# Second runs of a head pair: waiting output products ahead of the scores, and the runs planned nearer to the first

## The chip, the core and the metric

The kernel runs on one core of one Trainium2 chip. The metric is the device time of one execution in microseconds (us). The core's engines work side by side, each through its own queue in program order: TensorE (PE, matrix products into PSUM), VectorE (DVE), ScalarE (ACT), GpSimd (POOL, here mostly an issuer of weight loads) and SyncE (SP, an issuer of the other DMAs). They wait for each other through semaphores.

## The reference

One layer of a decoder trunk over 512 tokens with 1024 channels. Cut to what matters:

```
xn   = rmsnorm(x)
proj = xn @ w_in            # aq ak av ag | bq bf bi bg | gate_a gate_b
# attention branch: 8 heads x 64, blocks of 256, causal, relative-position bias
ya = attention(rmsnorm(aq), rmsnorm(ak), av, rel_bias)
ya = (ya * silu(ag)) @ w_up_a
# recurrence branch: 4 heads, key size 128, value size 128
yb = hgrn2(silu(bq), (1 - lb) * sigmoid(-bf), bi, log_decay(bf))
yb = (rmsnorm(yb) * silu(bg)) @ w_up_b
h  = x + (sigmoid(gate_a) * ya + sigmoid(gate_b) * yb) @ w_out
h  = h + (p @ w_ple) * sigmoid(h @ w_ple_gate)
```

All of it is held to float32 accuracy. With 512 tokens there are two key blocks and up to three chosen ones, so that every earlier block is always chosen and the attention is plain causal attention.

## The kernel before, in words

The large products (`mm3` at line 293, `prod_tok` at line 423) are each made of three products of rounded halves: high by high, high by low, low by high. A projection to 128 channels over all tokens is 24 matmuls of 128x512 and fills one PSUM bank. PSUM has 8 banks in three pools: "mm" (3 banks: the projections, one tile of the scores of a first run, and the attention's output `o`), "a" (3 banks: the scores `s`, and the recurrence's output `hop`) and "g" (2 banks: `lpb`, `lpa`, `hds` of the recurrence). A projection that needs a bank of "mm" waits until the last reader of the bank's previous content is through.

The weights of each projection are loaded by POOL or SP, rounded by ACT (`wh`, line 276) and completed by DVE (`wl`, line 277), two projections ahead.

The list `ORDER` sets the order of the projections while attention and recurrence run between them: bg, ag (gates of the two branches, `silu_block`), bf and bq (the recurrence's decay and query, `head`), ga and gb (the merge gates). `bf2` is the projection `bf` of recurrence head 2, and so on.

The order of TensorE's work is written out by a planner in the kernel. It keeps a clock `now` that `tick` moves on by 0.227 us for each matmul of a projection, and lets side generators go on when their due time has come: `attention`, `recurrence`, `hgrn_out` and others. `cost` adds time to the clock without running anything that is due. TensorE executes in exactly this order; the order on DVE, ACT, POOL and SP is made by a scheduler from it.

The attention works on four pairs of heads (0 to 3). A pair has two runs: the first (`STEPS[0]`) has the scores of query blocks 0, 1 and 2, the second (`STEPS[1]`) those of query block 3, six matmuls of line 815. After a run's scores come the softmax (DVE line 832, ACT lines 834 and 836, the transposition at DVE line 839) and 16 stores and regroupings of the probabilities through SP (line 850). `PACE` is the planned distance from one run to the next. The bias tiles of the next pair are loaded by SP (line 880, `bias`). After the next pair's first scores come the output products `o` of the pair before (line 863).

The recurrence works head by head. `hgrn_gates` makes of `bf` and `bq` the decay sums, keys and queries; ACT line 508 and DVE lines 512, 515 and 517 read the bank of `bf`, line 517 (`hk`) last. `hgrn_intra` prepares the inputs `hx` on DVE and ACT, waits for a run of the attention (`beside_attention`) and then issues the block products `lpb` and `lpa` (lines 592, 597, 563) right behind that run's scores. `hgrn_out` puts the head's output products (`hop`, lines 678 and 680: seven matmuls over four chunks of 128 tokens, each of which the profile records twice, since they are not of the rounded type) into the list `hops` for heads 0 to 2. Before the change that list is emptied at one place, in `hgrn_intra` of the next head, directly ahead of its block products:

```
        yield from beside_attention()
        while hops:
            hops.pop()()
        lpb = bank("g", f"lpb{h}")...
```

Line 695 (DVE) and line 692 (ACT) then read `hop`.

Of the kernel before, what the change touches and what calls it, by code (L numbers as in the profile page):

```python
# [28 lines left out]
LEVELS = (16, 8, 4, 2, 1)  # L29

STEPS = ((0, 1, 2), (3,))
PACE = (19.5, 22.5)

HP = 2.5
H0 = 8.0
# [33 lines left out]
def hybrid_layer_kernel(  # L69
# [32 lines left out]
    def bank(tag, name):  # L102
        return psum.tile([128, 512], F32, tag=tag, bufs={"mm": 3, "g": 2, "a": 3}[tag], name=name)
# [34 lines left out]
    def cost(us):  # L138
        now[0] += us
# [18 lines left out]
    def held_from(us, insts, until=None):  # L158

        def later():  # L160
            for inst in insts if until not in done else []:
                held(inst)
            yield 0.0

        spawn(later(), us)
# [331 lines left out]
    hops = []  # L497
# [290 lines left out]
    def attention(qn, kn, va, sags, res):  # L788
        def place(qb, j):

            return {0: (j, 0), 1: (2, 256 * j), 2: (j, 128), 3: (j, 0)}[qb]

        def tiles(step):
            return 2 + (len(STEPS[step]) > 1)
# [3 lines left out]
        def scores(hp, step):  # L798
            (qh, ql), (kh, kl) = qn[hp], kn[hp]
            nt = tiles(step)  # L800

            sps = [bank("a", f"s{hp}{step}{i}") for i in range(nt)]
            extra = bank("mm", f"s{hp}{step}x") if nt > 2 else None

            def where(qb, j):
                b_, o = place(qb, j)
                return (extra, 0) if (qb, j) == (1, 1) else (sps[b_], o)

            for qb in STEPS[step]:
                nk = 128 * (qb + 1)  # L810
                for i in range(3):
                    for j in range(2):
                        js = slice(64 * j, 64 * j + 64)
                        b_, o = where(qb, j)
                        PE.matmul(b_[:, o:o + nk], (qh, ql, qh)[i][js, qb * 128:qb * 128 + 128], (kh, kh, kl)[i][js, :nk],
                                  start=(i == 0), stop=(i == 2))
            cost(sum(3 * max(0.107, (qb + 1) * 0.0538) for qb in STEPS[step]))
            return where

        def softmax(hp, step, T, where):  # L820

            nt = tiles(step)
            z = pb[:, Z0[step]:Z0[step] + nt].rearrange("p t f -> p (t f)").rearrange("p (b t f) -> p b t f", b=4, t=nt)
            with tc.high_priority(offset=AHEAD):
                left = [sum(place(qb, j)[0] == b for qb in STEPS[step] for j in range(2)) for b in range(nt)]
                for qb, j in [(qb, j) for qb in STEPS[step] for j in range(2)]:
                    b_, o = place(qb, j)
                    nk = 128 * (qb + 1)
                    p_ = pb[:, b_, o:o + nk]
                    st = unit("ps", f"ps{hp}{qb}{j}", shape=(128, 4))  # L830
                    s_, so = where(qb, j)
                    in_order(V.tensor_tensor_reduce(p_, s_[:, so:so + nk], T[j][:, nk - 1::-1], -1.0, 3e38,  # L832
                                                    OP.add, OP.min, st[:, 0:1]))
                    A.activation(p_, p_, AF.Exp, bias=st[:, 0:1], scale=-1.0, accum_out=st[:, 1:2])  # L834
                    V.reciprocal(st[:, 2:3], st[:, 1:2])
                    A.activation(p_, p_, AF.Copy, scale=st[:, 2:3])  # L836
                    left[b_] -= 1
                    if left[b_] == 0:
                        V.transpose(z[:, :, b_, :].rearrange("p b (n c) -> p b n c", c=32),  # L839
                                    pb[:, b_].rearrange("p (n b c) -> p b n c", b=4, c=32))  # L840
            return z

        def sorted_groups(step, z):

            nt = tiles(step)
            pt = pb[:, PT0[step]:PT0[step] + nt].rearrange("p t f -> p (t f)").rearrange("p (a t f) -> p a t f", a=4, t=nt)
            with tc.high_priority(offset=AHEAD):
                for a in range(4):
                    for b in range(4):
                        nc.sync.dma_start(pt[32 * b:32 * b + 32, a], z[32 * a:32 * a + 32, b])  # L850
            return pt.rearrange("p a t (n c) -> p a (t n) c", c=32)

        def out_values(hp, pts):

            o = bank("mm", f"o{hp}")
            for step, pt in enumerate(pts):
                for qb in STEPS[step]:
                    qs = slice(qb * 128, qb * 128 + 128)
                    for kb in range(qb + 1):
                        for j in range(2):  # L860
                            h0 = hp * 128 + 64 * j
                            b_, o0 = place(qb, j)
                            PE.matmul(o[64 * j:64 * j + 64, qs], va[kb][:, h0:h0 + 64], pt[:, :, 4 * b_ + o0 // 128 + kb, :],
                                      start=(kb == 0), stop=(kb == qb))
            cost(1.5)
            sag = sags[hp]
            V.tensor_tensor(sag, o, sag, op=OP.mult)
            h_ = unit("A", f"yah{hp}", R)
            l_ = unit("A", f"yal{hp}", R)
            split(h_, l_, sag)  # L870
            res.append((h_, l_))
            done.add(f"ya{hp}")
# [3 lines left out]
        def bias(hp):  # L876
            for j in range(2):
                t = unit("T", f"bias{hp}{j}")
                row = ed[2 * hp + j:2 * hp + j + 1, :]
                held(nc.sync.dma_start(t, bass.AP(tensor=row.tensor, offset=row.offset, ap=[[1, 128], [1, 512]])))  # L880
                T[hp, j] = t
# [10 lines left out]
        for n in range(len(steps) + 1):  # L892
            ahead = BIAS if 0 < n < len(steps) and steps[n][1] == 0 else 0.0
            if n >= 1:
                yield PACE[steps[n - 1][1]] - ahead
            if ahead:
                bias(steps[n][0])
                yield ahead
            if n < len(steps):
                hp, i = steps[n]  # L900
                where = scores(hp, i)
            if n >= 1 and steps[n - 1][1] == NS - 1:
                ho = steps[n - 1][0]
                while f"ag{ho}" not in done:
                    yield lambda: f"ag{ho}" in done
                out_values(ho, [pts.pop(n - NS + i_) for i_ in range(NS)])
            if n < len(steps):
                z = softmax(hp, i, [T[hp, 0], T[hp, 1]], where)
                if others:
                    parts.clear()  # L910
                    others.pop()()
                    for n_, p_ in enumerate(list(parts)):
                        held_from(16.0 + 2.0 * n_, [p_])
                pts[n] = sorted_groups(i, z)
            runs[0] += 1
# [84 lines left out]
    spawn(qk_norm("q", proj_tok(0, "aq", xh, xl), qgain[:, 0:1], qn))  # L1000
    spawn(qk_norm("k", proj_tok(1, "ak", xh, xl), kgain, kn))
    spawn(attention(qn, kn, va, sags, ya))
    def up(i, n, ys, name):
        ws = weight(w_up[n, i])
# [341 lines left out]
```

## Time and profile before

| | |
|---|---|
| median of 3 runs | 452.07 us (450.89 to 452.41) |
| the profiled execution: its own time | 452.42 us |
| its span, from the first to the last instruction | 450.6 us |
| TensorE busy | 445.8 us, 99% of the span |
| VectorE, ScalarE, GpSimd busy | 334.6, 289.7, 59.9 us |
| mean granted TensorE clock | 0.999 |
| HBM read and written | 48.74 and 4.98 MB |

In the profile's rows a start time counts from the first instruction; the number behind it is the duration. Durations on TensorE overlap: the 128x512 matmuls take 0.39 us each and start 0.227 us apart. What a matmul costs is thus the distance to the next one's start. On DVE and ACT too the next instruction starts up to 0.1 us before the end of the one before, so that sums are made from starts to starts.

### The profile page before, as it was taken

The page shows a single profiled execution, that of the slowest core. Times are in us where ns is not written, and L with a number is a line of the kernel's source. Part 1 is how long each engine was busy: PE and PEld are TensorE (multiplying, and loading weights), DVE is VectorE, ACT ScalarE, POOL GpSimd, SP SyncE. Part 2 cuts the span into 40 slices and gives each one's busy share as a digit, 9 for nine tenths or more (in the row PEclk, how much of TensorE's full clock was granted, in tenths as well). Part 3 has the DMA queues.
Part 4 walks back from the last instruction along what each step waited for, and adds up shares of the span by engine and source line. Part 5 has one row for each costly group of instructions (what it writes and reads, how often), then busy time and mean ns, then how long its engine had stood idle before and what let it go on. Part 6 is the DMA issues. An engine that isn't in the chain of part 4 may idle for free.

```text
span 450.6 us, 8536 instructions
## 1 busy us (share of the span) xinstructions
PE 445.8 (99%) x3192; PEld 376.2 (83%) x3192; DVE 334.6 (74%) x682; ACT 289.7 (64%) x561; POOL 59.9 (13%) x97
## 2 busy tenths in 40 slices
PE   9999999999999999999999999999999999999996
PEld 8888888888878888878887888878888888899996
DVE  5869494776899797949857775465479868999844
ACT  5958474746689988979857996784135434555421
POOL 1000100000000101010100000111210103325520
PEclk9999999999999999999999999999999999999999
DMA  8802424168594455171425444265551444312111
GB/s 265 317 1 94 141 93 129 48 219 197 167 215 127 159 134 178 46 203 49 142 93 155 140 135 148 70 197 149 184 173 47 168 145 143 129 47 95 49 47 48
DMA packets 32857, 59.53 MB, mean 132 GB/s; under 512 B 7088, under 2 KB 18736, under 8 KB 32816
## 3 DMA queue, kind: packets, MB, share of 16 engines
q0 software_dynamic: 9056, 32.51, 22.5%
q1 hardware_dynamic: 23616, 26.47, 20.4%
q8 instruction: 25, 0.41, 0.4%
q14 instruction: 16, 0.13, 0.1%
q10 hardware_dynamic: 144, 0.01, 0.0%
HBM read 48.74 MB, written 4.98 MB: 119 GB/s over the span
## 4 chain that ended last, share of the span: by engine, by line
PE 89%; DVE 5%; SPq 2%; DMA 1%; issue 1%; ACT 0%; DVEq 0%
PE h L293 10%; PE g L1210 9%; PE ga L293 9%; PE gb L293 7%; PE ub L293 5%; PE aq L423 5%; PE ak L423 5%; PE ua L293 5%; PE av L423 5%; PE bf L293 5%; PE bi L423 5%; PE bq L293 4%; PE bg L293 4%; PE ag L293 4%; PE pe L293 2%; SPq L850 2%
## 5 line engine op out<-in xcount | busy, mean ns | idle before, releaser
L276 ACT ACTIVATE wh<-wf 128x1024 fp32r<-128x1024 f32 (+1 forms) x70 | 67.0, 958 | 63.2 <-issue 9.8
L277 DVE TENSOR_TENSOR wl<-wf,wh 128x1024 fp32r<-128x1024 f32 (+1 forms) x70 | 76.8, 1097 | 38.0 <-ACT wh L276 35.7
L266 POOL DMA_DIRECT2D wf<-in_w_tr_dram x30 | 15.8, 528 | 170.5 <-DVE wl L277 115.4
L293 PE MATMUL ga<-xh,wh 128*128 128x512 f32 x64 | 25.3, 396 | 0.4 <-DVE bg3s L491 0.4
L293 PE MATMUL gb<-xh,wh 128*128 128x512 f32 x64 | 25.0, 391 | 0.0
L293 PE MATMUL ga<-xh,wl 128*128 128x512 f32 x64 | 24.9, 390 | 0.0
L293 PE MATMUL ga<-xl,wh 128*128 128x512 f32 x64 | 24.9, 389 | 0.0
L293 PE MATMUL gb<-xl,wh 128*128 128x512 f32 x64 | 24.9, 389 | 0.0
L293 PE MATMUL h<-mh,wh 128*128 128x512 f32 x64 | 24.9, 389 | 0.0
L293 PE MATMUL h<-ml,wh 128*128 128x512 f32 x64 | 24.9, 389 | 0.0
L293 PE MATMUL h<-mh,wl 128*128 128x512 f32 x64 | 24.9, 389 | 0.0
L293 PE MATMUL gb<-xh,wl 128*128 128x512 f32 x64 | 24.9, 389 | 0.0
L834 ACT ACTIVATE pb<-pb,ps 128x128 f32<-128x128 f32 (+3 forms) x32 | 17.6, 551 | 10.0 <-DVE ps L832 10.0
L832 DVE CUSTOM_DVE_ANT_0 pb<-s,bias 128x128 f32<-128x128 f32 (+3 forms) x28 | 12.8, 493 | 7.1 <-DMA bias<-in_ed_dram 4.8
L1187 ACT ACTIVATE sg<-sg 128x256 f32<-128x256 f32 x12 | 5.0, 414 | 20.2 <-DVE sg L1184 20.2
L836 ACT ACTIVATE pb<-pb,ps 128x128 f32<-128x128 f32 (+3 forms) x32 | 16.0, 550 | 0.0
L542 ACT ACTIVATE hx<-hx 128x512 f32<-128x512 f32 x24 | 14.9, 623 | 1.4 <-DVE hx L541 1.3
L266 POOL DMA_DIRECT2D wf<-in_w_up_dram x16 | 8.6, 538 | 52.2 <-DVE wl L277 32.2
L839 DVE STREAM_TRANSPOSE pb<-pb 128x512 f32<-128x512 f32 x20 | 13.8, 696 | 2.0 <-ACT pb L836 2.0
L266 POOL DMA_DIRECT2D wf<-in_w_tok_dram x8 | 4.4, 549 | 80.2 <-DVE wl L277 68.2
L293 PEld LDWEIGHTS ga<-xh,wh 128*128 128x128 f32 x64 | 12.0, 188 | 3.5 <-DVE bg3s L491 0.8
L293 PEld LDWEIGHTS ga<-xh,wl 128*128 128x128 f32 x64 | 12.0, 188 | 2.6
(958 smaller groups left out, 1434.9 us busy)
## 6 DMA issues: line engine op xcount, KB each, us to landing
wf<-in_w_tr_dram POOLq DMA_DIRECT2D x30, 512.0 KB, 4.2
wf<-in_w_tok_dram POOLq DMA_DIRECT2D x8, 512.0 KB, 3.6
wf<-in_w_up_dram POOLq DMA_DIRECT2D x16, 256.0 KB, 3.0
wf<-in_w_o_dram POOLq DMA_DIRECT2D x8, 512.0 KB, 3.8
wf<-in_w_g_dram POOLq DMA_DIRECT2D x8, 512.0 KB, 3.6
wf<-in_w_tok_dram SPq DMA_DIRECT2D x6, 512.0 KB, 7.6
pb<-pb SPq DMA_DIRECT2D x64, 48.0 KB, 2.9
bias<-in_ed_dram SPq DMA_DIRECT2D x8, 256.0 KB, 4.1
```

The source lines that it names most:

```text
L266: (G if len(wraw) >= FAR else nc.sync).dma_start(raw, ap)
L276: rounds[i] = A.activation(hi, wraw[i], AF.Copy)
L277: V.tensor_tensor(lo, wraw[i], hi.bitcast(F32), op=OP.subtract)
L293: dense.append(PE.matmul(ps, a[:, k, :], b[k], start=(n == 0), stop=(n == tot - 1)))
L423: dense.append(PE.matmul(banks[t], a[:, s_], b[:, kk, :], start=(k == 0 and i == 0), stop=(k == KD - 1 and i == 2)))
L542: A.activation(x, x, AF.Exp)
L832: in_order(V.tensor_tensor_reduce(p_, s_[:, so:so + nk], T[j][:, nk - 1::-1], -1.0, 3e38, OP.add, OP.min, st[:, 0:1]))
L834: A.activation(p_, p_, AF.Exp, bias=st[:, 0:1], scale=-1.0, accum_out=st[:, 1:2])
L836: A.activation(p_, p_, AF.Copy, scale=st[:, 2:3])
L839: V.transpose(z[:, :, b_, :].rearrange("p b (n c) -> p b n c", c=32), pb[:, b_].rearrange("p (n b c) -> p b n c", b=4, c=32))
L850: nc.sync.dma_start(pt[32 * b:32 * b + 32, a], z[32 * a:32 * a + 32, b])
L1210: dense.append(PE.matmul(dst[i], a[:, k], b, start=(m == 0 and i in (1, 6, 5)), stop=(m == 11), skip_group_check=i not in (1, 6, 5)))
```

## The change

Two edits. The planned distance from a pair's first run to its second goes from 19.5 to 18.0 us. And where a second run (`i` is 1) is about to issue its scores, the list `hops` is emptied first, so that waiting output products of the recurrence stand ahead of the scores instead of behind them.

```
-PACE = (19.5, 22.5)
+PACE = (18.0, 22.5)
...
             if n < len(steps):
                 hp, i = steps[n]
+                while i and hops:
+                    hops.pop()()
                 where = scores(hp, i)
```

What this does to the order, at the places of which the prediction speaks. TensorE, second run of pair 0, before: `bf2` is the projection, `s010` and `s011` the scores of the pair's two heads, `hop0` the output products of recurrence head 0, and behind the rows shown come the block products `lpb1`.

```order
L293 MATMUL bf2_1555<-xh7_485,wl25_1475 128x512
L815 MATMUL s010_1580<-kh0_1130,qh0_877 128x512
L815 MATMUL s011_1581<-kh0_1130,qh0_877 128x512
L815 MATMUL s010_1580<-kh0_1130,ql0_881 128x512
L815 MATMUL s011_1581<-kh0_1130,ql0_881 128x512
L815 MATMUL s010_1580<-kl0_1134,qh0_877 128x512
L815 MATMUL s011_1581<-kl0_1134,qh0_877 128x512
L678 MATMUL hop0_1616<-sc_93,biv0_393 128x128 x2
L680 MATMUL hop0_1616<-ha0_609,st0_1095 128x128
L678 MATMUL hop0_1616<-sc_93,biv2_396 128x128
L680 MATMUL hop0_1616<-ha0_609,st0_1095 128x128
```

The same place after, up to the scores:

```order
L293 MATMUL bf2_1555<-xh5_452,wl25_1475 128x512
L678 MATMUL hop0_1574<-sc_93,biv0_393 128x128 x2
L680 MATMUL hop0_1574<-ha0_609,st0_1095 128x128
L678 MATMUL hop0_1574<-sc_93,biv2_396 128x128
L680 MATMUL hop0_1574<-ha0_609,st0_1095 128x128
L678 MATMUL hop0_1574<-sc_93,biv2_396 128x128
L680 MATMUL hop0_1574<-ha0_609,st0_1095 128x128
L815 MATMUL s010_1582<-kh0_1130,qh0_877 128x512
L815 MATMUL s011_1583<-kh0_1130,qh0_877 128x512
```

And where the block of small products ends, after:

```order
L563 MATMUL lpa1_1619<-hx1_16_1491 32x16 x16
L293 MATMUL bf2_1555<-xh6_460,wh25_1474 128x512
L293 MATMUL bf2_1555<-xl6_461,wh25_1474 128x512
L293 MATMUL bf2_1555<-xh6_460,wl25_1475 128x512
L293 MATMUL bf2_1555<-xh7_485,wh25_1474 128x512
L293 MATMUL bf2_1555<-xl7_486,wh25_1474 128x512
L293 MATMUL bf2_1555<-xh7_485,wl25_1475 128x512
L293 MATMUL bq2_1737<-xh0_412,wh26_1516 128x512
```

The whole block (scores, `hop`, `lpb`, `lpa`) stands six matmuls earlier, `hop0` ahead of the scores, and the last six matmuls of `bf2` come behind the block. In pairs 1 and 2 it is the same: the block stands six matmuls earlier (in pair 1 the last three of `bf3` come behind it, in pair 2 it now falls between `ga1` and `gb6`). In pair 3 `hops` is empty, and only the scores move, by six matmuls. The next pair's first run stands where it stood, since the 1.5 us that the planner counts for `hop` now fall into the distance.

DVE, second run of pair 1, before. Line 832 is the softmax's first step, `hu3`, `ha3` and `hk3` are the gates of recurrence head 3, which read the bank of `bf3`:

```order
L832 ISA pb_70,ps131_2237<-s111_2224,bias11_1863 128x512
L832 ISA ps131_2237 128x1
L512 TENSOR_SCALAR hu3_2411<-bf3_2188 128x512
L515 SCALAR_TENSOR_TENSOR ha3_2407<-bf3_2188,ha3_2407 128x512
L835 RECIPROCAL ps130_2231<-ps130_2231 128x1
L540 TENSOR_TENSOR hx2_8_2438<-hu2_1784 128x32x8
L541 TENSOR_TENSOR hx2_8_2438<-hu2_1784 128x32x8
L540 TENSOR_TENSOR hx2_4_2456<-hu2_1784 128x64x4
L541 TENSOR_TENSOR hx2_4_2456<-hu2_1784 128x64x4
L835 RECIPROCAL ps131_2237<-ps131_2237 128x1
L517 TENSOR_TENSOR hk3_2416<-ha3_2407,bf3_2188 128x512
```

After, from the softmax's transpositions on; between line 832 and these rows there now stand 15 others, the reduction of head 1's output (line 315), `wl35` and line 512 among them, and lines 695 and 313 stand ahead of line 832:

```order
L839 STREAM_TRANSPOSE pb_70<-pb_70 128x4x128 x2
L571 COPY_PREDICATED s322_2097<-mkf_69,lpb2_2283 128x64
L543 TENSOR_TENSOR hx2_4_2450<-hk2_1789,hx2_4_2450 128x64x4
L548 TENSOR_TENSOR hx2_4_2450<-ha2_1780,hx2_4_2450 128x64x4
L543 TENSOR_TENSOR hx2_2_2468<-hk2_1789,hx2_2_2468 128x128x2
L548 TENSOR_TENSOR hx2_2_2468<-ha2_1780,hx2_2_2468 128x128x2
L643 TENSOR_TENSOR ha2_1780<-ha2_1780,hu2_1784 128x384
L515 SCALAR_TENSOR_TENSOR ha3_2413<-bf3_2188,ha3_2413 128x512
L517 TENSOR_TENSOR hk3_2422<-ha3_2413,bf3_2188 128x512
```

Line 517, the last reader of the bank of `bf3`, had 8 instructions between the softmax's first step and itself, and now has 24, both transpositions among them. In pair 0 `hk2` moved likewise.

SP, the bias loads for pair 1, before (the 32x384 stores are those of pair 0's first run, the 32x256 ones those of its second):

```order
L850 DMA pb_70<-pb_70 32x384 x16
L1172 DMA pb_70<-in_pT_dram 128x512
L880 DMA bias10_1861<-in_ed_dram 128x512
L880 DMA bias11_1863<-in_ed_dram 128x512
L850 DMA pb_70<-pb_70 32x256 x16
```

After:

```order
L850 DMA pb_70<-pb_70 32x384 x16
L1174 DMA pb_70<-in_pT_dram 128x512
L850 DMA pb_70<-pb_70 32x256 x16
L880 DMA bias10_1861<-in_ed_dram 128x512
L880 DMA bias11_1863<-in_ed_dram 128x512
```

The two bias loads of pair 1 went behind the 16 stores of pair 0's second run. Those of pairs 2 and 3 keep their places; POOL's order is unchanged.

## The prediction

> **What bounds the kernel now.** I read the page first, for the share of the engines, and then the table of who TensorE waited for.
>
> ```profile
> PE 445.8 (99%) x3192; PEld 376.2 (83%) x3192; DVE 334.6 (74%) x682; ACT 289.7 (64%) x561; POOL 59.9 (13%) x97
> ```
> ```profile
> PE warm L193 <- PEq L1334: 0.8, 1, 0.8
> PE ga L293 <- DVE bg3s L491: 0.4, 1, 0.4
> ```
>
> TensorE is busy for 445.8 of 450.6 us, and all its waits in the table are two: 0.8 us at the start and one in the middle. So nothing that makes the attention or the recurrence ready earlier can shorten the kernel: TensorE has the same products to do either way. The time can change in three ways only: by what the edges between products of different shape cost, by the one stall going, and by new stalls. The one stall, in TensorE's timeline:
>
> ```profile
> 242.57 0.39 PE L293 MATMUL ga<-xh,wl 128*128 128x512 f32 x1
> 243.36 0.50 PE L293 MATMUL ga<-xh,wh 128*128 128x512 f32 x1 [0.40 <-DVE bg3s L491]
> ```
>
> The next matmul was due at 242.57 + 0.227 = 242.80 and started at 243.36: 0.56 us lost.
>
> **Edges between shapes.** Second run of pair 0 on TensorE, and the output products of head 3, which already stand between two projections:
>
> ```profile
> 152.17 0.39 PE L293 MATMUL bf<-xh,wl 128*128 128x512 f32 x1
> 152.49 0.50 PE L815 MATMUL s<-kh,qh 64*128 64x512 f32 x2
> 152.82 0.40 PE L815 MATMUL s<-kh,ql 64*128 64x512 f32 x2
> 153.06 0.40 PE L815 MATMUL s<-kl,qh 64*128 64x512 f32 x2
> 153.39 0.71 PE L678 MATMUL hop<-sc,biv 128*128 128x128 f32 x4
> 153.94 0.39 PE L680 MATMUL hop<-ha,st 128*128 128x128 f32 x2
> 154.83 0.39 PE L680 MATMUL hop<-ha,st 128*128 128x128 f32 x2
> 155.15 0.43 PE L592 MATMUL lpb<-hx 128*32 128x64 f32 x16
> ```
> ```profile
> 290.48 0.39 PE L293 MATMUL ga<-xh,wl 128*128 128x512 f32 x1
> 290.71 0.60 PE L678 MATMUL hop<-sc,biv 128*128 128x128 f32 x4
> 291.15 0.39 PE L680 MATMUL hop<-ha,st 128*128 128x128 f32 x2
> 292.18 0.48 PE L293 MATMUL ga<-xh,wh 128*128 128x512 f32 x1
> ```
>
> Entering the scores costs 0.32 - 0.23 = 0.09 us at the last projection matmul and another 0.33 - 0.24 = 0.09 in the first pair of scores. From scores to `hop` it is 0.33 - 0.24 = 0.09 and, in the first four records, 0.55 against the 0.44 of head 3 (290.71 to 291.15): 0.11. From `hop` to `lpb` it is 0.32 against 0.22 for two records. From a projection to `hop`, at head 3, it is nothing: 0.23 is the regular step. So in the new order (projection, `hop`, scores, `lpb`) the edge from scores to `hop`, 0.20 us, falls away. The edge into the scores is bought by `hop` instead of the projection. The edge from scores to `lpb` has no row; I take the 0.10 of `hop` to `lpb`, with 0.0 and 0.2 as bounds from the other edges. That is -0.2 us in each of pairs 0, 1 and 2: **-0.6 us** (-0.3 to -0.9). Splitting `bf2` and `bf3` adds nothing: the block had one edge from and one to a projection already. In pair 3 only the scores move.
>
> **What moves in time.** In pair 1 the block starts 6 x 0.227 = 1.36 us earlier. `hop` takes 1.47 us (290.71 to 292.18), so the scores come 1.47 + 0.1 - 1.36 = 0.2 us later than before, `hop` and `lpb` earlier. But the end of `bf3` now lies behind the block. It moves by the block's length, about 4 us (`s`, `hop` and the edges make 2.66 us up to 155.15, and `lpb` with `lpa` follow), and in pair 0 that of `bf2` likewise. Their readers follow. Below are TensorE's turns for three projections that need a bank which those readers or the gate `bg2` give back, with the start of pair 1's second run, then DVE's rows, then SP's issues:
>
> ```profile
> 167.50 0.39 PE L293 MATMUL gb<-xh,wh 128*128 128x512 f32 x1
> 194.88 0.39 PE L293 MATMUL bf<-xh,wh 128*128 128x512 f32 x1
> 201.09 0.50 PE L815 MATMUL s<-kh,qh 64*128 64x512 f32 x2
> 215.42 0.39 PE L293 MATMUL gb<-xh,wh 128*128 128x512 f32 x1
> ```
> ```profile
> 154.60 0.68 DVE L832 CUSTOM_DVE_ANT_0 pb<-s,bias 128x512 f32<-128x512 f32 x1
> 160.61 0.67 DVE L517 TENSOR_TENSOR hk<-ha,bf 128x512 f32<-128x512 f32 x1
> 178.62 0.29 DVE L832 CUSTOM_DVE_ANT_0 pb<-s,bias 128x128 f32<-128x128 f32 x1 [2.21 <-PE s L815]
> 191.42 0.68 DVE L491 TENSOR_TENSOR bg2s<-bg2s,bg 128x512 f32<-128x512 f32 x1
> 202.53 0.68 DVE L832 CUSTOM_DVE_ANT_0 pb<-s,bias 128x512 f32<-128x512 f32 x1
> 206.42 0.67 DVE L517 TENSOR_TENSOR hk<-ha,bf 128x512 f32<-128x512 f32 x1
> 207.01 0.74 DVE L695 SCALAR_TENSOR_TENSOR bg1s<-hop,sm,bg1s 128x512 f32<-128x512 f32 x1
> 208.29 0.25 DVE L602 TENSOR_TENSOR s<-lpb,mkf 128x128 f32<-128x128 f32 x1
> 210.39 0.68 DVE L519 TENSOR_TENSOR ha<-ha,hu 128x512 f32<-128x512 f32 x1
> 212.26 0.70 DVE L839 STREAM_TRANSPOSE pb<-pb 128x512 f32<-128x512 f32 x1
> 213.65 1.36 DVE L523 TENSOR_TENSOR_SCAN hu<-onec,ha 128x128 f32<-128x128 f32 x4
> 214.93 1.20 DVE L277 TENSOR_TENSOR wl<-wf,wh 128x1024 fp32r<-128x1024 f32 x1
> 216.18 0.54 DVE L643 TENSOR_TENSOR ha<-ha,hu 128x384 f32<-128x384 f32 x1
> 228.31 0.29 DVE L832 CUSTOM_DVE_ANT_0 pb<-s,bias 128x128 f32<-128x128 f32 x1 [3.24 <-DMA bias<-in_ed_dram]
> 230.21 0.29 DVE L832 CUSTOM_DVE_ANT_0 pb<-s,bias 128x128 f32<-128x128 f32 x1 [1.60 <-DMA bias<-in_ed_dram]
> ```
> ```profile
> 159.93 2.56 SPq L850 DMA_DIRECT2D pb<-pb  x4
> 163.16 0.90 SPq L880 DMA_DIRECT2D bias<-in_ed_dram  x2
> 165.87 10.75 SPq L850 DMA_DIRECT2D pb<-pb  x16
> 224.01 1.06 SPq L880 DMA_DIRECT2D bias<-in_ed_dram  x2
> ```
>
> **`gb5` behind `hk3`.** Three projections later `gb5` takes the bank of `bf3`. Before, line 517 ended at 206.42 + 0.67 = 207.09 for a turn at 215.42: 8.3 us to spare. Now its place on DVE is behind nearly everything that filled the idle-free stretch from 202.53 to 214.93. Of these 12.4 us, lines 695 and 313 (207.01 to 208.29, 1.3) now lie ahead of line 832, and line 519 (0.6) and the four scans (1.3) stay behind line 517. New ahead of it are a `wl` (1.15) and line 643 (0.5) with a small reduction (0.1). Line 517 therefore ends about 12.4 - 1.3 - 1.9 + 1.8 = 11.0 us after line 832 starts. Lines 695 and 313 now follow `hop`, which ends at 201.09 - 1.36 + 1.47 = 201.2, and ACT's squaring of it; with some 0.7 for that and 1.3 for themselves line 832 starts at 203.2, or at 204.5 if ACT is a microsecond late. That gives 214.2 to 215.5. The turn comes at 215.42 less the 0.4 saved at two edges, 215.0. The cover of 8.3 us is used up: -0.8 to +0.5, and ACT, which has to deliver four more results in this stretch, can only add; I take **+0.4 us** (0 to 1.2).
>
> **`gb2` behind `hk2`.** The same in pair 0, without the four products `hx_4` and `hx_2` and line 643 (1.8 us) ahead of line 517: some 9.3 us from line 832 at 155.0, so 164.3. The first transposition also waits for stores of the first run, which SP had issued by 159.93 + 2.56 = 162.5; nine instructions, 4.3 us by the same count, follow: 167. The turn is 167.50 - 0.2. **+0.1 us** (0 to 0.7).
>
> **`bf3` behind `bg2`.** Here SP's queue decides. Pair 1's bias was issued at 163.16, and the softmax at 178.62 found it there and waited for the scores. Now it is queued behind 16 stores, which take 10.75 us and start when pair 0's second transposition ends, at 165.9 before and by the count above at about 166.4. So it is issued at 177.1. In pair 2 this order already stands: issue at 224.01, softmax at 228.31 and 230.21, 4.3 us and 1.9 more. So pair 1's softmax starts at 181.4, some 2.8 to 4.4 us late, I take 3.2. From line 832 to line 491 DVE ran without idle (178.62 to 191.42), so the delay arrives whole. Line 491 had ended at 192.10 for `bf3`'s turn at 194.88 less 0.2: 2.6 us to spare. **+0.6 us** (0 to 1.8).
>
> **`ga1` behind `bg3`.** This is the present stall of 0.56, at the end of the same path in pair 2: bias issued at 224.01 behind stores that begin at the end of the second transposition (212.26). That transposition now follows line 832 after 12.4 - 1.3 - 1.9 - 3.2 (rows that went behind it) + 1.3 (the new `wl` and reduction) = 7.3 us instead of 9.7. From 203.2 to 204.5 it starts at 210.5 to 211.8, 0.5 to 1.8 earlier: **-0.5 us** (0 to -0.56).
>
> The sum: -0.6 + 0.4 + 0.1 + 0.6 - 0.5 = 0.0, with ends at -1.5 and +3.4. Against the profiled execution's own 452.42 us, of which 1.8 lie around the span, that is 452.4. The median of the runs shown is 452.07, 0.35 lower, so I forecast **452.1 us**, and 451.2 to 453.1 if no term reaches its end.
>
> **Rivals.**
>
> **Nothing new stalls** (faster, 451.0). If `gb2`, `gb5` and `bf3` all get their banks in time, -0.6 and -0.5 remain, -1.1. For it: my count puts two of the three within 0.5 us of no stall. Against: two covers, 8.3 and 6.2 us (167.50 less 161.28), both shrink to nothing by the same count.
>
> **The late bias decides** (slower, 454.2). The place is SP's queue ahead of pair 1's first run. If both bias tiles come as late as the second did in pair 2, the softmax is 4.4 us late, `bf3` waits 1.8, and since ACT's and DVE's queues stay behind, `gb5` waits its 1.2: -0.6 - 0.5 + 1.8 + 1.2, and 0.2 at `gb2`, make +2.1. It decides once line 491 of `bg2` ends after 196. For it: the order shows the move, and pair 2 shows the wait of 3.24 and 1.60. Against: DVE idles 2.21 us ahead of 178.62, slack that a late DVE would eat first, and pair 2, with the full wait, lost only 0.56.
>
> The Trainium skill, "Perfetto Trace Analysis", section "Optimizing Tensor Performance", says that independent groups of matmuls should rotate through different PSUM banks so that emptying one bank overlaps the next group's products. A projection cut in two, with its readers pushed back, works against that; by this rule the time would be that of this rival. The trace agrees so far that the kernel's one stall is a projection that waits for a bank.
>
> **Nearer runs shorten the attention** (faster, 450.7 or less): four runs, 1.36 us each, would be up to 5.4 us if the attention set the end. Against: TensorE idles 0.4 us outside its start, and the first runs keep their places.
>
> **How the numbers follow.** The forecast gets 0.55, nothing new stalls 0.25, the late bias 0.18, the shorter attention 0.02. About 0.3% of 452.07, 1.36 us, is what a measurement of this kernel can tell from no change, since its own three runs spread over 1.5. Faster by more than that needs nearly all of the gains and no stall, or the last rival: 0.09. Slower needs the late bias, or the forecast's terms together at their upper ends: 0.19. The rest, 0.72, is the same. The range leaves out one tenth on either side: 450.8 at the low end, a little under the first rival's time, and 453.9 above, between the forecast's upper end and the second rival.
>
> **What would show it.** TensorE's rows in pairs 0 to 2 should show a regular step of 0.23 from the projection into `hop`, and a scores-to-`lpb` edge of about 0.1. The waits of TensorE should no longer name `bg3s`, and name `hk` (line 517) for `gb` and `bg2s` (line 491) for `bf`. SP should issue pair 1's bias at about 177, and DVE line 832 should wait for it until about 181. I am wrong if line 517 of head 3 ends much before 214, if line 832 of pair 1 does not wait for the bias, or if TensorE's waits in the middle sum to more than 2.5 us.

## The result: 5 us slower

| | before | after |
|---|---|---|
| median, 6 runs each | 451.91 us (450.89 to 452.41) | 457.07 us (456.06 to 457.81) |
| ratio to before, 95% interval | | 1.0114 (1.0097 to 1.0131) |
| span of the profiled execution | 450.6 us | 455.4 us |
| TensorE busy | 445.8 us | 446.6 us |

The forecast was 452.1 us with a range up to 453.9; the time lies 3.2 us above the range. The ratios here and below leave out runs more than 1.5% above the fastest of their kernel, which is one run in all (461.47 us, in run 11). The page of the changed kernel, and its table of what TensorE waited for:

```profile
PE 446.6 (98%) x3192; PEld 376.7 (83%) x3192; DVE 334.5 (73%) x682; ACT 289.1 (63%) x561; POOL 60.0 (13%) x97
```
```profile
PE gb L293 <- ACT hu L514: 1.5, 1, 1.5
PE gb L293 <- DVE hk L517: 1.0, 1, 1.0
PE ag L293 <- DVE ps L832: 1.0, 1, 1.0
PE bf L293 <- DVE bg2s L491: 0.9, 1, 0.9
PE warm L193 <- PEq L1336: 0.8, 1, 0.8
```

TensorE has the same work; the stall that named `bg3s` is gone, and four others have come. TensorE's timeline has them at `gb2`, `ag2`, `bf3` and `gb5`:

```profile
168.88 0.47 PE L293 MATMUL gb<-xh,wh 128*128 128x512 f32 x1 [1.01 <-DVE hk L517]
186.59 0.51 PE L293 MATMUL ag<-xh,wh 128*128 128x512 f32 x1 [0.97 <-DVE ps L832]
198.69 0.50 PE L293 MATMUL bf<-xh,wh 128*128 128x512 f32 x1 [0.92 <-DVE bg2s L491]
219.08 0.39 PE L293 MATMUL gb<-xh,wl 128*128 128x512 f32 x1
220.97 0.47 PE L293 MATMUL gb<-xh,wh 128*128 128x512 f32 x1 [1.50 <-ACT hu L514]
```

A step is 0.23 where nothing waits. From the matmul before, `gb5` took 220.97 - 219.08 = 1.89, so 1.66 were lost; in the same way 1.17 at `gb2`, 1.14 at `ag2` and 1.08 at `bf3`, 5.0 in all. The row of `gb5` names line 514, which ended last (220.88 in ACT's rows below) but does not read the bank; the last reader is line 517, whose end at 220.82 stands in DVE's rows.

**A measure for the experiments.** The time up to the first matmul of `bf2` varies between the profiled executions of this study by 2.7 us (146.35 to 149.09), although the program is the same there. So I also compare the **middle**, from the first matmul of `bf2` to the first of `gb7`, which holds all that the change moves ahead of pair 3. In TensorE's timeline, of the kernel before and of the changed one:

```profile
146.96 0.39 PE L293 MATMUL bf<-xh,wh 128*128 128x512 f32 x1
258.60 0.39 PE L293 MATMUL gb<-xh,wh 128*128 128x512 f32 x1
```
```profile
147.19 0.40 PE L293 MATMUL bf<-xh,wh 128*128 128x512 f32 x1
263.38 0.39 PE L293 MATMUL gb<-xh,wh 128*128 128x512 f32 x1
```

111.64 before, 116.19 after: +4.55. The four stalls are +5.05 and the stall at `ga1` is gone, -0.56; the three blocks, each from the last projection matmul ahead of it to the first behind it, are together 0.35 shorter (12.65 against 13.00), and steps a little longer than 0.227, most of them the first behind a stall, make up the 0.4 that is left.

### The profile page after: what moved, and what is told of

The parts are those of the page before. It is cut to its first block, busy times and chain, and to the rows that moved or that the text cites. A ratio compares the mean times of both kernels' runs of the same rounds, so it can differ in the third digit from the quotient of the medians.

```text
span 455.4 us, 8530 instructions
## 1 busy us (share of the span) xinstructions
PE 446.6 (98%) x3192; PEld 376.7 (83%) x3192; DVE 334.5 (73%) x682; ACT 289.1 (63%) x561; POOL 60.0 (13%) x97
## 4 chain that ended last, share of the span: by engine, by line
PE 77%; issue 13%; ACT 3%; DMA 3%; DVE 1%; POOL 1%; POOLq 0%; DVEq 0%; ACTq 0%
PE ga L293 10%; PE h L293 10%; PE g L1212 9%; PE ub L293 5%; PE aq L423 5%; PE ak L423 5%; PE ua L293 5%; PE av L423 5%; PE bi L423 4%; PE gb L293 4%; DMA wf<-in_w_tr_dram 3%; PE ag L293 2%; PE bg L293 2%; PE bf L293 2%; PE pe L293 2%
## 5 line engine op out<-in xcount | busy, mean ns | idle before, releaser
L293 PEld LDWEIGHTS gb<-xh,wh 128*128 128x128 f32 x64 | 12.0, 188 | 5.7 <-ACT hu L514 3.3
```

The costliest lines, as they stand in the source:

```text
L293: dense.append(PE.matmul(ps, a[:, k, :], b[k], start=(n == 0), stop=(n == tot - 1)))
```

## Where the four stalls come from

Pair 1's second run in the changed kernel, first ACT's timeline, then DVE's:

```profile
203.42 1.06 ACT L276 ACTIVATE wh<-wf 128x1024 fp32r<-128x1024 f32 x1 [2.58 <-DMA wf<-in_w_tr_dram]
206.29 0.58 ACT L692 ACTIVATE ho<-hop 128x512 f32<-128x512 f32 x1
213.38 0.72 ACT L836 ACTIVATE pb<-pb,ps 128x512 f32<-128x512 f32 x1
218.52 0.71 ACT L510 ACTIVATE ha<-ha,onec 128x512 f32<-128x512 f32 x1
220.08 0.80 ACT L514 ACTIVATE hu<-hu,onec,lb 128x512 f32<-128x512 f32 x1
```
```profile
206.90 0.75 DVE L695 SCALAR_TENSOR_TENSOR bg1s<-hop,sm,bg1s 128x512 f32<-128x512 f32 x1 [1.17 <-ACT ho L692]
208.19 0.65 DVE L832 CUSTOM_DVE_ANT_0 pb<-s,bias 128x512 f32<-128x512 f32 x1
214.85 1.28 DVE L839 STREAM_TRANSPOSE pb<-pb 128x512 f32<-128x512 f32 x2
217.40 0.43 DVE L543 TENSOR_TENSOR hx<-hk,hx 128x256 f32<-128x256 f32 x1 [1.09 <-ACT hx L542]
219.41 0.68 DVE L515 SCALAR_TENSOR_TENSOR ha<-bf,ha 128x512 f32<-128x512 f32 x1
220.13 0.69 DVE L517 TENSOR_TENSOR hk<-ha,bf 128x512 f32<-128x512 f32 x1
```
```profile
205.81 0.40 PE L815 MATMUL s<-kl,qh 64*128 64x512 f32 x2
```

The scores are done at 206.2 (last row). The softmax, line 832, starts at 208.19, since `hop`'s readers, lines 695 and 313, stand in front of it on DVE and wait for ACT, which has a late weight tile (line 276, 2.58 us for its load) and the gate of `gb3` in front of line 692. All else in this stretch is queued behind: the transpositions, which follow ACT's line 836 at 213.38, the gates, of which ACT's line 510, needed by line 515, runs only at 218.52, and through the stores SP's issue of the next bias. In pair 0 it is the same, with one wait more: the first transposition stands in front of the gates and waits for the first run's stores. DVE in pair 0, a weight load that POOL issued at that time, SP, and DVE in pair 1's first run:

```profile
164.50 0.71 DVE L839 STREAM_TRANSPOSE pb<-pb 128x512 f32<-128x512 f32 x1 [2.22 <-DMA pb<-pb]
168.07 0.66 DVE L517 TENSOR_TENSOR hk<-ha,bf 128x512 f32<-128x512 f32 x1
```
```profile
160.27 0.53 POOL L266 DMA_DIRECT2D wf<-in_w_tr_dram  x1 [9.19 <-DVE nms L320]
```
```profile
168.11 11.00 SPq L850 DMA_DIRECT2D pb<-pb  x16
179.15 1.05 SPq L880 DMA_DIRECT2D bias<-in_ed_dram  x2
```
```profile
183.63 0.29 DVE L832 CUSTOM_DVE_ANT_0 pb<-s,bias 128x128 f32<-128x128 f32 x1 [3.98 <-DMA bias<-in_ed_dram]
185.54 0.29 DVE L832 CUSTOM_DVE_ANT_0 pb<-s,bias 128x128 f32<-128x128 f32 x1 [1.62 <-DMA bias<-in_ed_dram]
```

The stores that SP issued from 157.4 to 159.9 landed 1.9 us later each; those issued from 160.5 to 162.4, beside that weight load, took 2.6 to 3.9 us. In the trace the transposition starts as the store issued at 160.53 has landed (164.48). That the load is what slowed the stores is my reading of the times; no run changes the load alone.

Three causes can be behind all this, and the trace alone doesn't part them: (1) pair 1's bias behind the 16 stores; (2) the block inside `bf2` and `bf3`, so that the gates come behind the block's work; (3) `hop` ahead of the scores, so that `hop`'s readers come ahead of the softmax. I ran each alone and in pairs.

## The experiments

Each ratio is to the kernel before, measured beside it, with its 95% interval; "middle" is against 111.64 and comes from one profiled execution each. Runs 6 and 8, which fit no row, have a middle of +1.15 and -0.13.

| bias of pair 1 | block | on TensorE first | median us | ratio | middle |
|---|---|---|---|---|---|
| behind | early | hop (the change) | 457.07 | 1.0114 (1.0097 to 1.0131) | +4.55 |
| ahead | early | hop | 454.35 | 1.0046 (1.0028 to 1.0063) | +1.62 |
| ahead | late | hop | 453.17 | 1.0014 (0.9998 to 1.0031) | +0.43 |
| behind | early | scores | 452.24 | 1.0000 (0.9984 to 1.0017) | -0.37 |
| ahead | early | scores | 452.47 | 1.0004 (0.9991 to 1.0017) | -0.26 |
| behind | late | scores | 454.13 | 1.0033 (1.0012 to 1.0054) | +0.77 |
| behind | early | hop, its readers behind the softmax | 452.19 | 0.9984 (0.9966 to 1.0001) | -0.73 |
| ahead | early | hop, its readers behind the softmax | 451.69 | 0.9986 (0.9972 to 1.0000) | -0.59 |
| ahead | late | hop, its readers behind the softmax | 452.38 | 0.9999 (0.9985 to 1.0013) | -0.28 |

**1. The change with the bias ahead of the stores.**

```
-BIAS, BIAS0 = 8.0, 4.0
+BIAS, BIAS0 = 10.0, 4.0
```

> The changed kernel with pair 1's two bias tiles issued on SP ahead of the 16 stores of pair 0's second run again, as in the kernel before (BIAS 10.0 for 8.0; the bias of pairs 2 and 3 stays behind the stores; all TensorE, DVE and ACT orders of the changed kernel stay). Theory 1 (the late bias makes the stalls of ag2, 1.14 us, and of bf3, 1.08 us): the softmax of pair 1's first run waits for its scores only, both stalls go, the stalls of gb2 and gb5 (1.17 and 1.66) stay: 457.1 - 2.2 = 454.9 us, 454.5 to 455.3. Rival (everything on DVE is late there because hop's work and the gates were pushed, the bias is only the name on the wait): ag2 and bf3 still stall by over 0.5 each, 456 to 457.

454.35 us, 0.15 under theory 1's range and far from the rival's. `ag2` and `bf3` no longer wait, `gb2` loses 1.43 (1.17 in the change) and `gb5` 0.83 (1.66); what TensorE still waits for in the middle is, in its table (the second row is `gb5`, again under the name of the event that came last):

```profile
PE gb L293 <- DVE hk L517: 1.3, 1, 1.3
PE gb L293 <- ACT ny L305: 0.7, 1, 0.7
```

So the late bias makes two of the four stalls and half of a third, given all the rest.

**2. hop first, the block at its old place.**

```
-PACE = (18.0, 22.5)
+PACE = (19.5, 21.0)
```

> Hop stands in front of the scores as in the changed kernel, but the second run's block is back at its old place: bf2 and bf3 are complete ahead of it (PACE 19.5, 21.0 for 18.0, 22.5). On DVE the gates' last lines hk2 and hk3 then stand ahead of the transpositions again, and on SP the bias of pairs 1 and 2 ahead of the 16 stores. Theory 2 (bf2 and bf3, cut by the block, hold their banks until the gates are through, and that stalls gb2 and gb5): both stalls go, with the bias ahead ag2, bf3 and ga1 have none either; the edges leave -0.6 and the old stall's 0.56 goes: 451.9 - 1.1 = 450.8 us, 450.4 to 451.6. Theory 3 (it is hop ahead of the scores that makes DVE and ACT late): gb2 and gb5 still wait, some 1.2 and 1.7, 453.2 to 454.5.

453.17 us, above theory 2's range and below theory 3's. `gb2` and `gb5` have their banks in time, as theory 2 says, but something neither had foreseen took the gain:

```profile
PE o L863 <- DMA pb<-pb: 0.9, 2, 0.6
```

The output products of pairs 0 and 1 now wait for the stores of a late softmax, 0.9 us in all, which the missing stall at `ga1` and the shorter edges make up in part. So `hop` first makes the softmax late here too; it only meets another consumer.

**3. and 4. The block early, the scores first; the bias behind the stores, and ahead of them.** Of the change's diff only the first line is made, with the sum of the distances kept:

```
-PACE = (19.5, 22.5)
+PACE = (18.0, 24.0)
```

> The other half: the second run's block starts six matmuls earlier, inside bf2 and bf3, as in the changed kernel, but the scores stand in front of hop as in the kernel before (PACE 18.0, 24.0, no early hop). Pair 1's bias stands behind the 16 stores as in the changed kernel. Theory 2: gb2 and gb5 wait by over 1 us each, and with theory 1 ag2 and bf3 by about 1 each, and the edges save nothing: 456.0 to 457.8 us. Theory 3: gb2 and gb5 have their banks in time, only ag2 and bf3 stall: 453.6 to 454.6.

> As the run with the block early and the scores in front of hop, with pair 1's bias ahead of the 16 stores. It leaves the early block alone, without hop's move and without the late bias. Theory 2: gb2 and gb5 still wait over 1 us each, ag2 and bf3 do not: 454.0 to 455.6 us. Theory 3: no new stall is left, 451.5 to 452.5. If theory 1 is wrong, ag2 and bf3 still stall and this run is not faster than the one with the bias behind.

452.24 and 452.47 us: no loss at all, and no wait in the middle in either; run 3 comes out below both ranges given, run 4 in that of theory 3. Theory 2 falls: `bf2` and `bf3` are cut just as in the change, and line 517 of head 3 comes in time. And the late bias, which made two stalls in the change, makes none here. DVE in run 3:

```profile
200.99 0.68 DVE L832 CUSTOM_DVE_ANT_0 pb<-s,bias 128x512 f32<-128x512 f32 x1
211.99 0.68 DVE L517 TENSOR_TENSOR hk<-ha,bf 128x512 f32<-128x512 f32 x1
```

From line 832 to the end of line 517 it is 11.7 us here and 12.6 in the change. The stretch is not much shorter; it starts earlier. What remained was theory 3, in the form that what counts is how late the softmax is.

**5. The change, with hop's readers behind the softmax on DVE and ACT.** TensorE's order is that of the changed kernel, instruction for instruction, and SP's too.

```
+ e_ = A.activation(p_, p_, AF.Exp, ...)          # line 834
+ soft[:] = [e_, r_]                              # r_: line 832
...
+ sq_ = A.activation(o, op_, AF.Square); h < GH - 1 and behind(sq_, soft[0])
+ g_ = V.scalar_tensor_tensor(sbg[h], op_, ...); h < GH - 1 and behind(g_, soft[1])
```

> The changed kernel with TensorE's order untouched (hop ahead of the scores, block inside bf2 and bf3, bias behind the stores), but on ACT and DVE hop's readers (lines 692 and 695, with line 313) are tied behind the softmax's first steps (lines 834 and 832) of the same run. What has been measured so far: the early block alone costs nothing (452.24, 452.47) and hop first alone almost nothing (453.17); both together cost 5 us. Theory 4a (the second run's softmax is late because hop's readers stand ahead of it on DVE and ACT, and the gates and transpositions behind it follow): line 832 starts about 1.3 us earlier, the stalls of gb2, ag2, bf3 and gb5 go or fall below 0.3 each, 452.0 to 453.2 us. Theory 4b (the scores' 1.5 us on TensorE are enough, the readers don't matter): at least gb2 and gb5 still wait about 1 us each, 454.5 to 457.

452.19 us: the whole loss is gone, with the bias still behind the stores and the block still inside `bf2` and `bf3`. Its ratio of 0.9984 (0.9966 to 1.0001) can't be told from no change. Its table of TensorE's waits has one row, the start, and this is DVE in pair 1:

```profile
PE warm L193 <- PEq L1336: 0.8, 1, 0.8
```
```profile
202.78 0.69 DVE L832 CUSTOM_DVE_ANT_0 pb<-s,bias 128x512 f32<-128x512 f32 x1 [2.66 <-PE s L815]
205.55 0.75 DVE L695 SCALAR_TENSOR_TENSOR bg1s<-hop,sm,bg1s 128x512 f32<-128x512 f32 x1
207.48 0.70 DVE L839 STREAM_TRANSPOSE pb<-pb 128x512 f32<-128x512 f32 x1
214.47 0.68 DVE L517 TENSOR_TENSOR hk<-ha,bf 128x512 f32<-128x512 f32 x1
```

The softmax starts when the scores end, and the transposition 4.7 us after it instead of 6.7. Line 517 ends at 215.15. That is 0.6 before TensorE's turn at 215.76, so there is little to spare, but enough. Theory 4a holds: with TensorE's and SP's orders as in the change, it is the order on DVE and ACT, set by the place of `hop`'s readers, that costs the time. The scores' 1.5 us on TensorE alone cost nothing that shows. What the run does not part is the readers' own time from what else the scheduler moved with them. In pair 0 the softmax came only 1.1 us earlier (153.90 for 154.97), but the completion of a weight tile (line 277) came 1.8 us later (160.60 for 158.76), so that POOL issued the next weight load at 162.12 instead of 160.27 and only the last of the first run's stores landed late; the transposition did not have to wait at all.

**6. The change with the gates ahead of the transpositions on DVE.**

```
+ turn.append(V.transpose(z[...], pb[...]))                        # line 839
...
+ k_ = V.tensor_tensor(kb, a, F, op=OP.subtract); [behind(t_, k_) for t_ in turn if h > 1]   # line 517
```

> The changed kernel with TensorE's order untouched, but on DVE the second run's two transpositions (line 839) are tied behind line 517 of the gates (hk2, hk3), the last reader of bf2 and bf3. SP's order follows: pair 1's and pair 2's bias stand ahead of the 16 stores again. To be compared with the run that has the bias ahead alone (454.35, gb2 1.42 and gb5 0.83 late). If the wait of the transposition for the stores of the first run, in front of the gates on DVE, is what makes line 517 late in pair 0, gb2's stall goes; gb5's falls by the two transpositions, 1.3, and goes too: 452.0 to 453.0 us, less what the later stores make out_values wait (0.4 and 0.6 in the run with hop first and the block late). If ACT's order sets line 517 (line 515 waits for line 510), gb2 and gb5 still wait by over 0.8 each: 454 to 455.

453.62 us, between the two. In pair 0 the transposition's wait in front of the gates was the cause, as the expectation's first case has it: `gb2` no longer waits. In pair 1 ACT's order sets line 517: DVE waited 1.40 for its line 542 in front of line 517, and `gb5` still lost 0.79. And the transpositions, now last, make pair 1's `o` wait 0.9:

```profile
212.66 0.42 DVE L543 TENSOR_TENSOR hx<-hk,hx 128x256 f32<-128x256 f32 x1 [1.40 <-ACT hx L542]
```
```profile
216.22 0.47 PE L293 MATMUL gb<-xh,wh 128*128 128x512 f32 x1 [0.63 <-ACT hu L514]
230.44 1.09 PE L863 MATMUL o<-pb,avv 128*64 128x128 f32 x16 [0.86 <-DMA pb<-pb]
```

**7. The kernel before with the bias behind the stores.** TensorE's order is untouched.

```
-BIAS, BIAS0 = 8.0, 4.0
+BIAS, BIAS0 = 6.0, 4.0
```

> The kernel before with pair 1's two bias tiles behind the 16 stores on SP (BIAS 6.0 for 8.0) and TensorE's order untouched: the late bias alone. Theory 1 alone (a bias behind the stores stalls ag2 and bf3): issue at about 177, landing at 181.5 and 183.4, softmax 2.9 to 4.6 us late, bf3 0.5 to 1.1 and ag2 0.5 to 1.1 late: 453.0 to 454.0 us. Rival (the bias is late enough only where the second run's softmax, and with it the stores, are late as well, as the run with the early block and the bias behind suggests, which had no stall): 451.7 to 452.6.

454.13 us, 0.1 above theory 1's range. But the stalls are not those it named. Line 832 of pair 1 started at 180.87 for the first bias tile and at 181.49 for the second, 2.3 and 2.7 late; `ag2` lost nothing and `bf3` 0.1. The delay went on to pair 1's second run, whose stores hold up pair 2's bias, and landed at `ga1`, where 1.0 was lost in place of 0.56:

```profile
PE ga L293 <- DVE bg3s L491: 0.8, 1, 0.8
```

The middle is 0.77 longer, about half of what the medians differ by. The profiled execution itself took 452.78, 1.35 below the median, so the other half can't be placed.

**8. The first line of the change alone, distances 18.0 and 22.5.** The sum is 1.5 smaller than in run 3, so later runs stand nearer too.

> The first line of the change alone (PACE 18.0, 22.5), scores in front of hop: second runs stand six matmuls nearer to the first, and as the sum of the two distances is smaller by 1.5, all later runs stand nearer as well. By the run with the early block (452.24) no new stall: 451.5 to 452.7 us. If nearer first runs make the second runs' banks and buffers collide, over 453.

454.07 us, ratio 1.0032 (1.0005 to 1.0058), over the 453 of the second case. But its middle is 0.13 shorter than before, so its profile shows no loss that the edit makes; it shows 1.45 lost at `bf2`, ahead of anything moved, behind a weight load that came 2.5 us late (ACT and DVE carry the 2.5 us unchanged to line 491, which started at 148.35 for 145.85 before). Its ten runs lie between 451.8 and 457.2; the two longest, 457.1 and 457.2, are the only ones with a mean granted clock of 0.994 and 0.995 instead of 0.998 or more, of which the last section tells more. Whether such late loads were chance or are made likelier by the shorter distance stays open.

**9. and 10. hop's readers behind the softmax, with the block late; with the bias ahead.** The edits are those of run 5 with that of run 2, and of run 5 with that of run 1.

> Hop ahead of the scores on TensorE, the block at its old place behind bf2 and bf3 (PACE 19.5, 21.0), and hop's readers tied behind the softmax's first steps on DVE and ACT. Against the run with hop first and the block late (453.17, out_values of pairs 0 and 1 waited 0.4 and 0.6 for the stores of a late softmax): by theory 4a the softmax comes about 1 us earlier, these two waits go or halve, and the four edges and ga1's 0.56 stay gained: 451.2 to 452.2 us, at or up to 0.3% under the kernel before. If the scores' 1.5 us on TensorE make the stores late by themselves, both waits stay: 452.8 to 453.6.

> The run with the softmax first on DVE and ACT (452.19), with pair 1's bias ahead of the 16 stores as well. In that run the bias landed 0.7 to 1.4 us after the scores and no projection waited for it, so by theory 4a nothing is left to gain: 451.6 to 452.5 us, the same as without. If the late bias costs time by another way than a wait of TensorE, under 451.4.

452.38 and 451.69 us. With the block late the waits of `o` shrank from 0.9 to 0.2, as theory 4a had it; the median came out 0.2 above its range and can't be told from the kernel before. With the bias ahead nothing more is gained than in run 5: its median is the lowest of the study, but its ratio of 0.9986 is no better than run 5's 0.9984, and neither can be told from no change. Runs 5, 9 and 10 differ from the change, run 2 and run 1 by the tied readers alone, and the tie takes 5.3, 0.7 and 2.2 us from the middle.

**11. The changed kernel once more.**

> The changed kernel as it is, once more, beside the two others on one chip: 456 to 458 us, 4.5 to 5.5 above the kernel before, and the same four stalls (gb2, ag2, bf3, gb5) within 0.5 us each. If its loss were a matter of one chip or of the weight loads of one execution, it would come out below 455 or with other stalls.

456.75 us, ratio 1.0085 (1.0055 to 1.0115), the same four stalls: the loss is no matter of one chip. `gb5` did not keep to its 0.5: it lost 3.4, behind a weight load 4.2 us late, with a consequence told in the last section.

## Why the prediction was wrong, point by point

**What bounds the kernel** was right: TensorE's work is the same, the loss is four waits, and all four are projections that wait for a bank.

**Edges, -0.6.** Right in kind. TensorE in pair 0 after the change:

```profile
151.06 0.39 PE L293 MATMUL bf<-xh,wl 128*128 128x512 f32 x1
151.29 0.60 PE L678 MATMUL hop<-sc,biv 128*128 128x128 f32 x4
153.51 0.40 PE L815 MATMUL s<-kl,qh 64*128 64x512 f32 x2
153.84 0.43 PE L592 MATMUL lpb<-hx 128*32 128x64 f32 x16
```

Projection to `hop` is the regular 0.23, scores to `lpb` 0.33, an edge of 0.10 as assumed, and from the last projection to `lpb` it is 2.78 against 2.98 (152.17 to 155.15): -0.20. In pairs 0 and 1 the stretch of `lpb` and `lpa` gave some of it back (perhaps since it now stands nearer to what it waits for): the blocks took 4.27, 4.25 and 4.13 us against 4.33 each before, -0.35 over the three pairs in the change and -0.5 in runs 9 and 10.

**`gb2` behind `hk2`, +0.1: measured 1.17.** The term was mis-sized at the stores of the first run, which were taken as done when SP had issued them, by 162.5. The transposition waits for their landing, and started at 164.50, 2.0 later. The store it waited for landed 3.9 us after its issue, twice as long as the ones before it. Line 832 (154.97 for the 155.0 counted) and the 4.3 us behind the transposition (164.50 to 168.73) were right.

**`gb5` behind `hk3`, +0.4 (0 to 1.2): measured 1.66.** The mechanism and the line are right. Line 832 started at 208.19, or 204.2 if the 3.95 us that TensorE was late by then are taken off (the last matmul ahead of the block started at 203.36, for 200.77 - 1.36 = 199.41), inside the range given (203.2 to 204.5). From there to the end of line 517 it took 12.6 against 11.0 counted: ACT, of which the prediction said that it "can only add", is what I take the other 1.6 to be: it ran the weights, `bf3`'s first gate and the norm in front of line 836, and DVE idled 1.09 for its line 542 (the row of line 543).

**`bf3` behind `bg2`, +0.6: measured 1.08, and `ag2` 1.14 unforeseen.** SP issued the bias at 179.15, not 177.1, since the stores began 1.7 us later than counted; and the second tile, 1.9 us behind the first, counts for line 491. The prediction had both rows of pair 2, saw a delay of 2.8 to 4.4 us, and took 3.2, nearer to the first tile's. `ag2` was missed altogether: it takes the bank of "mm" that holds one tile of the first run's scores, and its reader is the softmax itself. Before, that reader ended at 179.82, 4.2 ahead of `ag2`, as DVE's and TensorE's rows of the kernel before show:

```profile
179.40 0.42 DVE L832 CUSTOM_DVE_ANT_0 pb<-s10x,bias 128x256 f32<-128x256 f32 x1
```
```profile
183.98 0.40 PE L293 MATMUL ag<-xh,wh 128*128 128x512 f32 x1
```

**`ga1`, -0.5:** right, 0.56 gone.

**The step that failed** is what the prediction counted behind line 832, not the start of that line. It saw that lines 695 and 313 would stand ahead of it, priced this at 2 us, and line 832 started where it said in both pairs. By its own count the covers of 8.3 and 6.2 us, and the 2.6 us of `bf3`, were then used up, so that whatever was missing went into TensorE's time. Three things were. The wait of the first transposition was counted from the issue of the stores and not from their landing (2.0 us: `gb2` 1.17 instead of 0.1, and through the stores behind it 1.7 us of the bias's delay, so that `bf3` lost 1.08 instead of 0.6). The bank of `ag2` had no term (1.14). And the stretch from line 832 to the end of line 517 was counted too short, most likely for ACT's part in it (12.6 instead of 11.0, and 12.6 again in run 6, where DVE waited in it for ACT: `gb5` 1.66 instead of 0.4). Together the three stalls that it had and the one that it had not came to 5.05 instead of 1.1.

What the runs add is that no one of the three changes makes this by itself. Without the late softmax the cut projections and the late bias together cost nothing (run 3), and the late bias alone makes the middle 0.77 longer, 0.44 of it at `ga1` (run 7); with `hop` first and the block late the middle is 0.43 longer (run 2); with `hop` first and the block early it is 1.62 longer (run 1), and with the late bias as well 4.55. Tying `hop`'s readers behind the softmax removes the whole loss (run 5).

**The rivals.** "The late bias decides" had the place and the sign and gave 454.2; the bias does make two stalls (run 1), but makes them only because the second run ahead of it is late (runs 3 and 5). The rule that was set beside it, from the Trainium skill, "Perfetto Trace Analysis", section "Optimizing Tensor Performance", that groups of matmuls should rotate through PSUM banks so that emptying one overlaps the next, agrees with the trace so far that every new wait is a projection waiting for a bank or for what empties it. "Nothing new stalls" was run 5's course: it gave -1.1, and run 5's middle is -0.73. "Nearer runs shorten the attention" has nothing for it: from the first matmul of `gb7` to the end both kernels take 192.0 us (450.6 - 258.60 and 455.4 - 263.38).

**The signs.** Of what was to show, the edges, the names of the waits, and the bias's wait came, SP's issue at 179.15 for 177 and line 832 at 183.63 for 181. Of the three signs of being wrong one came: TensorE's waits in the middle sum to 4.4 us in its table, over the 2.5 allowed.

## To carry to other kernels

When products are moved ahead on one engine, see where their readers go on the others: here they went ahead as well, and the more urgent reader stood behind them in the queue. Keep the order of the readers by urgency, apart from that of the products (run 5 got back 5 us by tying two instructions of each pair). Where a count leaves a cover at nothing, every small thing that it left out is paid for in full, so ask what else stands in that stretch. Where a wait is for a transfer, count from its landing, and ask which other transfer runs beside it; and look at every pool from which the late result holds a buffer, not only at those the change names.

## What the runs showed of the hardware

**A wait of 3 us also took the clock.** In run 11's profiled execution TensorE started nothing for 3.59 us ahead of `gb5` (3.20 of them idle by the profile), and then ran at half speed. The windows (columns: stretch, its length, busy time and instructions of PE, PEld, DVE, ACT and POOL, granted clock, DMA share, GB/s) and TensorE's rows:

```profile
219.00:222.40 3.40, 0.20 (x2) 0.09 (x1) 3.26 (x8) 3.40 (x8) 0.00 (x0) 0.88 0.21 48
225.00:228.00 3.00, 3.00 (x8) 2.32 (x7) 2.04 (x7) 2.77 (x9) 0.53 (x1) 0.50 0.70 217
```
```profile
218.75 0.39 PE L293 MATMUL gb<-xh,wl 128*128 128x512 f32 x1
222.34 0.77 PE L293 MATMUL gb<-xh,wh 128*128 128x512 f32 x1 [3.20 <-ACT ny L305]
223.75 0.63 PE L293 MATMUL gb<-xh,wh 128*128 128x512 f32 x1
228.44 0.39 PE L293 MATMUL gb<-xh,wl 128*128 128x512 f32 x1
```

From 222.34 to 228.44 the step is 0.43 in place of 0.23, at a granted clock of 0.50: 6.1 us, of which some 2.9 are lost beside the wait's 3.4. The stalls of 1.9 and less in the other profiles were not followed by this: behind these stalls their granted clock stays at 1.00. The Trainium skill, "TensorE: Matmul & The Clock Gate", section "Part 1: The HAM clock gate", states that TensorE falls to half its clock after an idle window of about 3.4 us and that back-to-back matmuls of 512 columns then start 426.7 ns apart; the trace agrees with the second, and here an idle time of 3.2 us in the profile was enough. This fits the spread of run 11 from 454.1 to 461.5, where the kernel before lay between 451.2 and 454.1: the three longest of its eleven runs (459.6, 460.9 and 461.5) have a mean granted clock of 0.993 to 0.996, the other eight, up to 456.9, of 0.998 or more. The stall that led to it is seen in the profiled execution alone.

**Leaving one product kind for another has a price by pair.** Projection to `hop` costs nothing, as the prediction's rows had it; scores to `lpb`, for which it had no row and took 0.10, cost 0.10. One edge less is 0.20 for a block that nothing else disturbs (4.13 against 4.33).
